# A two-layer hybrid encoder on one core: the attention's last products (weights times values) take precedence over other TensorE work

## The chip, the cores and the metric

One core of a Trainium2 chip runs the whole program in one launch. The metric is the device time of one execution in microseconds (us); a verdict of faster or slower is given from 2% on. TensorE is called PE here, VectorE DVE, ScalarE ACT, GpSimd POOL, and SP is the engine whose queue issues the loads and stores.

## The reference, cut to what matters

```python
for l in range(2):                                   # x is 512 x 1024, float32
    h = rmsnorm(x, g_mix_pre[l])
    a.., b.., c.. = split(h @ w_in[l])
    o_a = gated_deltanet(...)                        # 4 heads of 128, chunks of 64
    o_b = dsa_attention(q, k, v, qi, ki, wi)         # 4 heads of 64, 4 blocks of 128 queries
    o_c = hgrn2(...)                                 # 4 heads of 64
    x = x + rmsnorm(concat([o_a, o_b, o_c]) @ w_out[l], g_mix_post[l])
    h = rmsnorm(x, g_ffn_pre[l])
    x = x + rmsnorm(conv_geglu_ffn(h, ...), g_ffn_post[l])

# of dsa_attention, for one block of 128 queries
score = einsum('bqhs,bqh->bqs', relu(einsum('bqhd,bsd->bqhs', qib, ki)), wib)
_, idx = top_k(score, 128)                           # keys kept for each query
p = softmax(where(valid, q @ k[idx] * 64 ** -0.5, -inf))
o = einsum('bqhk,bqkd->bqhd', p, v[idx])             # weights times values
```

The last line is what the change is about. The kernel computes it with a mask in place of the gather.

## The kernel before

Activations stand with features on partitions and 512 tokens along the free axis. A projection (`project`, lines 179 to 181) multiplies in three passes, high by high, low by high and high by low parts, each a 128x512 product, into a tile `p_mm`; the output projection and the second half of the feed-forward network (`down`, lines 218 to 224) do the same into `p_dn`. These two are called the wide products below.

Each layer runs a mixing part (`mix_phase`) and a feed-forward part. The mixing part computes the projections, the attention (`dsa_*`), the delta rule (`dn_all`) and the gated recurrence (`hg_tile`). `dsa_attend` works on the query blocks in the order 0, 2, 3, 1; block b sees b+1 blocks of 128 keys. For its four heads it computes logits (`p_logit`), the softmax, a transpose of the weights on PE (`p_pT`, line 416) with a copy back by ACT into `lg` (line 417), and then the last products: 4(b+1) of them, 128x128 moving by 64 columns, summed in the tile `p_dsao` (line 420). ACT copies that into `ob` (line 423).

`dn_all` inverts triangular 64x64 blocks from 16x16 pieces: DVE makes `ut` (lines 552, 556) from a piece `u` that SP loads (line 549), PE multiplies 32x32 blocks (`p_l`, 64 of them at line 567 and 64 at 575, with DVE's `z` between, line 568), then 591, 603, 605, 614 and 620, with copies by DVE and ACT between. The recurrence of the delta rule over four chunks follows (`p_u`, `p_S`, `p_dno`, `p_kS`), and next to it the gated recurrence (`hX`, `hkh`, `hqh`, `p_h`, `p_hlo`, lines 693 to 830).

The code is written for a scheduler (the tile framework) that puts each engine's instructions into one fixed order before the run: it takes, of the instructions that are ready by its own account, the one with the best priority. Priority follows the order of the code, and `first(n)` puts what is emitted inside it ahead by `n * 3000` places. Weight splits, evictions of projections and norms already stand in `first`. At run time each engine works its list in that order and waits on semaphores. Wide products that are ready fill the places between the products of the chains.

Places where the order before is shown have lines of the kernel before; the changed kernel has one line more from line 419 on.

Of the kernel before, what the change touches and what calls it, by code (L numbers as in the profile page):

```python
# [19 lines left out]
P = 128  # L20
# [18 lines left out]
def hybrid_encoder_kernel(ctx: ExitStack, tc: tile.TileContext, x, win, wout, wup, wdn, gall, gates,  # L39
                          dncw, ffcw, vecs, hglb, consts, out):  # L40
    nc = tc.nc
    V, S, G, PE, SP = nc.vector, nc.scalar, nc.gpsimd, nc.tensor, nc.sync
# [6 lines left out]
    def first(n=1):  # L49
        return tc.high_priority(offset=n * FIRST)  # L50
# [204 lines left out]
    def mix_phase(l, hid):  # L255
        def alloc(pool, name, tag=None, bufs=1, n=T, dt=F32):
            return pool.tile([P, n], dt, name=name, tag=tag or name, bufs=bufs)

        with ExitStack() as outer:
# [32 lines left out]
            def misc_proj(a):  # L292
                mf = alloc(pool, "mf", tag="hraw", bufs=6)
                with first():
                    S.activation(mf, a, AF.Copy)
                p = ds("misc")
                for b in range(NB):
                    PE.transpose(p[:, b * P:(b + 1) * P], mf[:, b * P:(b + 1) * P], ident)
                mt = alloc(pool, "mt")
                S.activation(mt, p, AF.Copy)  # L300
                return mt.rearrange("p (b c) -> p b c", b=NB)
# [27 lines left out]
            def stacked(a, s, cols, keys, n):  # L329
                PE.matmul(a[:, :n], s[:, cols], keys[0][:, :n], start=True, stop=False)  # L330
                PE.matmul(a[:, :n], s[:, cols], keys[1][:, :n], start=False, stop=True)
# [63 lines left out]
            def dsa_attend(sp, b, qq, keys, misc, bias):  # L395
                n = (b + 1) * P
                qs = slice(b * P, (b + 1) * P)
                lgs = []
                mxs = tiny([4], "mxs")
                for h in range(4):  # L400
                    a = ds("logit")
                    stacked(a, qq[h], qs, keys, n)
                    lg = alloc(sp, "lg", bufs=4)
                    V.tensor_tensor_reduce(lg[:, :n], a[:, :n], bias, 1.0, -3.0e38, OP.add, OP.max, mxs[:, h:h + 1])
                    lgs.append(lg)
                V.tensor_scalar(mxs, mxs, -0.125, None, op0=OP.mult)
                sums = tiny([4], "sums")
                for h in range(4):
                    S.activation(lgs[h][:, :n], lgs[h][:, :n], AF.Exp, scale=0.125, bias=mxs[:, h:h + 1],
                                 accum_out=sums[:, h:h + 1])  # L410
                V.reciprocal(sums, sums)
                for h in range(4):
                    V.tensor_scalar(lgs[h][:, :n], lgs[h][:, :n], sums[:, h:h + 1], None, op0=OP.mult)
                    p = ds("pT")
                    for j in range(b + 1):
                        PE.transpose(p[:, j * P:(j + 1) * P], lgs[h][:, j * P:(j + 1) * P], ident)
                    S.activation(lgs[h][:, :n], p[:, :n], AF.Copy)
                po = po_("dsao")
                for j, h in ((j, 2 * i + r) for i in range(2) for j in range(b + 1) for r in range(2)):
                    PE.matmul(po[64 * (h % 2):64 * (h % 2) + 64, (h // 2) * P:(h // 2 + 1) * P],  # L420
                              misc[:, j, 0:64], lgs[h][:, j * P:(j + 1) * P], start=j == 0, stop=j == b)
                pv = po[:, :2 * P].rearrange("p (i t) -> p i t", i=2)
                S.activation(ob[:, :, qs], pv, AF.Copy)

# [409 lines left out]
            misc = misc_proj(am)  # L834
# [5 lines left out]
            with tc.tile_pool(name="dsa", bufs=1, reuse_waits="tile") as sp:  # L840
                qi = dsa_stack(sp, 0, a0) + dsa_stack(sp, 1)
                keys, ikeys = dsa_keys(sp)
                bias = {0: cst[:, C_B0:C_B0 + P]}
                scores = (None for b in (3, 2, 1) for _ in dsa_score(sp, b, qi, ikeys, cols_[0], bias))
                qq = []
                units = dn_proj()
                for c in DSA_ORDER:
                    if c == "s":
                        next(scores)
                    elif c == "q":  # L850
                        qq += dsa_stack(sp, 4 + len(qq) // 2)
                    else:
                        ts = next(units)
                for _ in scores:
                    pass
                oa = dn_all(ts, cols_)
                for b in (3, 2, 1):
                    dsa_select(bias[b])
                for b in (0, 2, 3, 1):
                    dsa_attend(sp, b, qq, keys, misc, bias[b])  # L860
# [176 lines left out]
```

## Time and profile before

| | us |
|---|---|
| median of the timed runs | 1434.95 |
| the three runs | 1419.99, 1436.18, 1434.95 |
| the profiled execution's own time | 1422.91 |
| its span, first to last instruction | 1420.9 |
| mean granted clock of PE in it | 0.986 |

[...] Durations of PE's products are modelled and overlap: in a row of wide products the next one starts about 0.23 us after the one before, though each is given 0.39 us. An instruction of the code with full float32 operands shows as two records in the profile, so 64 products are 128 records.

### The profile page before, as it was taken

The numbers are of one execution on the slowest core, as the hardware profiler recorded it, in microseconds if no ns is written. First come the engines' busy times: TensorE is split into PE (matmuls) and PEld (weight loads), VectorE is DVE, ScalarE is ACT, GpSimd is POOL, SyncE is SP. The second block draws the span as 40 slices with busy tenths as digits, with TensorE's granted clock in tenths as the row PEclk, the third lists the DMA queues.
The fourth block names the chain that finished last, engine by engine and source line by source line (L and its number), as shares of the span: only waits on it lengthen the run. The fifth ranks groups of instructions, "written<-read, shape, count | busy, mean of one in ns | idle before, by whom it ended". The sixth has DMA issues, their size and how long they took to land.

```text
span 1420.9 us, 19912 instructions
## 1 busy us (share of the span) xinstructions
PE 1372.2 (97%) x7692; PEld 1128.5 (79%) x7692; DVE 912.8 (64%) x1671; ACT 683.9 (48%) x1287; POOL 114.6 (8%) x94
## 2 busy tenths in 40 slices
PE   6999999999999999999999999899999999999998
PEld 6887777778888888888788777688788888888886
DVE  5599977977566656423646998749666665664233
ACT  4355866565444444313543577645554344443132
POOL 2031220110000000000022221102000000000000
PEclk9999999999999999999999999869999999999999
DMA  4423220134423232323333323201353323232332
GB/s 169 124 93 111 94 72 17 60 134 153 161 89 104 91 103 92 102 92 114 136 105 100 97 92 93 56 1 60 133 186 114 103 91 104 89 104 89 104 104 89
DMA packets 50959, 142.93 MB, mean 101 GB/s; under 512 B 14321, under 2 KB 15281, under 8 KB 50865
## 3 DMA queue, kind: packets, MB, share of 16 engines
q1 hardware_dynamic: 50864, 141.66, 30.6%
q8 instruction: 61, 1.00, 0.3%
q14 instruction: 34, 0.27, 0.1%
HBM read 129.29 MB, written 8.95 MB: 97 GB/s over the span
## 4 chain that ended last, share of the span: by engine, by line
PE 75%; DVE 16%; ACT 5%; issue 3%; DMA 1%; DVEq 0%; ACTq 0%
PE p_mm L180 15%; PE p_mm L181 15%; PE p_mm L179 14%; PE p_dn L223 7%; PE p_dn L224 7%; PE p_dn L218 7%; DVE sc L392 3%; DVE m L391 2%; DVE qkv L198 2%; PE p_tp L172 1%; PE p_dsao L420 1%; DVE wlo L123 1%; PE p_hlo L780 1%; ACT whi L122 1%; ACT junk L473 1%
## 5 line engine op out<-in xcount | busy, mean ns | idle before, releaser
L179 PE MATMUL p_mm<-hhi,whi 128*128 128x512 f32 (+1 forms) x1232 | 472.4, 384 | 4.0 <-DVE qkv L198 3.8
L180 PE MATMUL p_mm<-hlo,whi 128*128 128x512 f32 (+1 forms) x1232 | 471.9, 383 | 0.5 <-DVE hlo L176 0.4
L181 PE MATMUL p_mm<-hhi,wlo 128*128 128x512 f32 (+1 forms) x1232 | 472.0, 383 | 0.0
L123 DVE TENSOR_TENSOR wlo<-wraw,whi 128x1024 fp32r<-128x1024 f32 x166 | 204.2, 1230 | 306.1 <-ACT whi L122 304.7
L122 ACT ACTIVATE whi<-wraw 128x1024 fp32r<-128x1024 f32 x190 | 201.4, 1060 | 299.1 <-PE p_mm L180 155.6
L179 PEld LDWEIGHTS p_mm<-hhi,whi 128*128 128x128 f32 x1232 | 233.2, 189 | 47.7 <-ACT qkv L196 4.4
L180 PEld LDWEIGHTS p_mm<-hlo,whi 128*128 128x128 f32 x1232 | 233.4, 189 | 42.6 <-DVE hlo L176 1.1
L181 PEld LDWEIGHTS p_mm<-hhi,wlo 128*128 128x128 f32 x1232 | 233.5, 189 | 42.2 <-issue 0.7
L198 DVE SCALAR_TENSOR_TENSOR u<-p_mm,fcw,u 128x511 f32<-128x511 f32 (+1 forms) x172 | 128.4, 746 | 3.0
L218 PE MATMUL p_dn<-whi,ah 128*128 128x512 f32 x272 | 105.8, 389 | 0.0
L223 PE MATMUL p_dn<-wlo,ah 128*128 128x512 f32 x272 | 105.8, 389 | 0.0
L224 PE MATMUL p_dn<-whi,al 128*128 128x512 f32 x272 | 105.8, 389 | 0.0
L122 ACT ACTIVATE ah<-u 128x512 fp32r<-128x512 f32 x44 | 27.8, 632 | 122.1 <-DVE u L921 122.1
L123 POOL TENSOR_TENSOR wlo<-wraw,whi 128x1024 fp32r<-128x1024 f32 x24 | 57.6, 2400 | 244.6 <-PE p_mm L181 93.0
L920 ACT ACTIVATE u<-u 128x512 f32<-128x512 f32 x44 | 27.8, 633 | 91.8 <-DVE u L198 91.8
L224 PEld LDWEIGHTS p_dn<-whi,al 128*128 128x128 f32 x272 | 51.1, 188 | 10.7
L218 PEld LDWEIGHTS p_dn<-whi,ah 128*128 128x128 f32 x272 | 51.1, 188 | 10.6
L223 PEld LDWEIGHTS p_dn<-wlo,ah 128*128 128x128 f32 x272 | 51.1, 188 | 10.6
L196 ACT ACTIVATE u<-p_mm,fcw 128x512 f32<-128x512 f32 x86 | 57.5, 669 | 0.0
L198 DVE SCALAR_TENSOR_TENSOR qkv<-p_mm,cw,qkv 128x511 f32<-128x511 f32 (+2 forms) x72 | 53.0, 739 | 5.2 <-ACT qkv L196 4.8
L391 DVE MAX8 m<-sc 128x8 f32<-128x512 f32 (+2 forms) x96 | 52.8, 554 | 1.0
L392 DVE MATCH_REPLACE8 sc<-m,sc 128x512 f32<-128x512 f32 (+2 forms) x96 | 51.9, 542 | 0.0
(292 smaller groups left out, 1862.7 us busy)
## 6 DMA issues: line engine op xcount, KB each, us to landing
wraw<-in_wup_dram SPq DMA_DIRECT2D x88, 512.0 KB, 3.4
wraw<-in_win_dram SPq DMA_DIRECT2D x60, 512.0 KB, 3.5
wraw<-in_wdn_dram SPq DMA_DIRECT2D x44, 512.0 KB, 3.4
wraw<-in_wout_dram SPq DMA_DIRECT2D x16, 512.0 KB, 3.4
xd<-xb SPq DMA_DIRECT2D x12, 512.0 KB, 2.7
xb<-xd SPq DMA_DIRECT2D x12, 512.0 KB, 5.5
xb<-in_x_dram SPq DMA_DIRECT2D x8, 512.0 KB, 6.0
g<-in_gall_dram SPq DMA_DIRECT2D x8, 512.0 KB, 4.8
```

Source lines behind the costliest of these rows:

```text
L122: S.activation(hi, src, AF.Copy)
L123: eng.tensor_tensor(lo, src, hi.bitcast(F32), op=OP.subtract)
L179: PE.matmul(out_, ah, bh, start=start, stop=False)
L180: PE.matmul(out_, ah, bl, start=False, stop=False)
L181: return PE.matmul(out_, al, bh, start=False, stop=stop)
L196: S.activation(dst, acc, AF.Copy, scale=w[:, taps - 1:taps])
L198: V.scalar_tensor_tensor(dst[:, s:], acc[:, :T - s], w[:, taps - 1 - s:taps - s], dst[:, s:], op0=OP.mult, op1=OP.add)
L218: first = PE.matmul(acc[b], th[:, bs], piece(hi, i, T), start=k == 0, stop=False)
L223: PE.matmul(acc[b], th[:, bs], piece(lo, i, T), start=False, stop=False)
L224: PE.matmul(acc[b], tl[:, bs], piece(hi, i, T), start=False, stop=k == 2 * npair - 1)
L391: V.max(m8, bias)
L392: V.match_replace(bias, m8, bias, REPL)
```

## The change

The loop of the last products of `dsa_attend` is put inside `first(2)`, so that the scheduler ranks them 6000 places further ahead than before. No instruction, operand or buffer is added or taken away.

```diff
                 po = po_("dsao")
-                for j, h in ((j, 2 * i + r) for i in range(2) for j in range(b + 1) for r in range(2)):
-                    PE.matmul(po[64 * (h % 2):64 * (h % 2) + 64, (h // 2) * P:(h // 2 + 1) * P],
-                              misc[:, j, 0:64], lgs[h][:, j * P:(j + 1) * P], start=j == 0, stop=j == b)
+                with first(2):
+                    for j, h in ((j, 2 * i + r) for i in range(2) for j in range(b + 1) for r in range(2)):
+                        PE.matmul(po[64 * (h % 2):64 * (h % 2) + 64, (h // 2) * P:(h // 2 + 1) * P],
+                                  misc[:, j, 0:64], lgs[h][:, j * P:(j + 1) * P], start=j == 0, stop=j == b)
```

Three places show what the scheduler makes of it.

The first is PE's list in the first layer, at the attention of query block 3 (16 last products, `p_dsao`). Before:

```order
L416 MATMUL p_pT<-cst,lg 128x128 x8
L179 MATMUL p_mm<-hhi,whi 128x512
L180 MATMUL p_mm<-hlo,whi 128x512
L420 MATMUL p_dsao<-lg,mt 64x128
L181 MATMUL p_mm<-hhi,wlo 128x512
L420 MATMUL p_dsao<-lg,mt 64x128 x2
L416 MATMUL p_pT<-cst,lg 128x128 x8
L420 MATMUL p_dsao<-lg,mt 64x128 x13
L330 MATMUL p_logit<-kh,qs 128x256
L331 MATMUL p_logit<-kl,qs 128x256
```

And in the change:

```order
L416 MATMUL p_pT<-cst,lg 128x128 x8
L180 MATMUL p_mm<-hlo,whi 128x512
L421 MATMUL p_dsao<-lg,mt 64x128
L181 MATMUL p_mm<-hhi,wlo 128x512
L179 MATMUL p_mm<-hhi,whi 128x512
L421 MATMUL p_dsao<-lg,mt 64x128 x7
L416 MATMUL p_pT<-cst,lg 128x128 x8
L180 MATMUL p_mm<-hlo,whi 128x512
L181 MATMUL p_mm<-hhi,wlo 128x512
L421 MATMUL p_dsao<-lg,mt 64x128
L330 MATMUL p_logit<-kh,qs 128x256
L331 MATMUL p_logit<-kl,qs 128x256
```

The products of the first two heads now stand together ahead of the second batch of transposes, where most of them stood behind it; 7 of the last 8 stand behind the first pair of logits of the next block.

The second place is PE's list in the first layer some 50 rows later, where `dn_all` begins its 32x32 products. Nothing there is inside `first(2)`; its order changes because the scheduler's choices further up changed. Before:

```order
L181 MATMUL p_mm<-hhi,wlo 128x512
L179 MATMUL p_mm<-hhi,whi 128x512
L567 MATMUL p_l_1405<-ut,Mt 32x32 x32
L567 MATMUL p_l_1439<-ut,Mt 32x32 x32
L575 MATMUL p_l_1473<-ut,z_1045 32x32 x32
L180 MATMUL p_mm<-hlo,whi 128x512
L575 MATMUL p_l_1508<-ut,z_1045 32x32 x32
L591 MATMUL p_l_1550<-tt,Mt 32x32 x8
L181 MATMUL p_mm<-hhi,wlo 128x512
L179 MATMUL p_mm<-hhi,whi 128x512
```

And in the change:

```order
L181 MATMUL p_mm<-hhi,wlo 128x512
L568 MATMUL p_l_1405<-ut,Mt 32x32 x32
L568 MATMUL p_l_1439<-ut,Mt 32x32 x32
L576 MATMUL p_l_1473<-ut,z_1045 32x32 x32
L576 MATMUL p_l_1508<-ut,z_1045 32x32 x32
L592 MATMUL p_l_1550<-tt,Mt 32x32 x8
L179 MATMUL p_mm<-hhi,whi 128x512
L180 MATMUL p_mm<-hlo,whi 128x512
L181 MATMUL p_mm<-hhi,wlo 128x512
```

The wide product between the two halves of the second batch has left; 136 small products follow each other with no wide one among them.

The third place is the same one in the second layer, on PE. Before:

```order
L179 MATMUL p_mm<-hhi,whi 128x512
L180 MATMUL p_mm<-hlo,whi 128x512
L567 MATMUL p_l_7310<-ut,Mt 32x32 x32
L567 MATMUL p_l_7344<-ut,Mt 32x32 x32
L575 MATMUL p_l_7378<-ut,z_6952 32x32 x32
L575 MATMUL p_l_7413<-ut,z_6952 32x32 x32
L181 MATMUL p_mm<-hhi,wlo 128x512
L591 MATMUL p_l_7455<-tt,Mt 32x32 x8
L179 MATMUL p_mm<-hhi,whi 128x512
```

And in the change:

```order
L568 MATMUL p_l_7310<-ut,Mt 32x32 x32
L568 MATMUL p_l_7344<-ut,Mt 32x32 x32
L179 MATMUL p_mm<-hhi,whi 128x512
L180 MATMUL p_mm<-hlo,whi 128x512
L181 MATMUL p_mm<-hhi,wlo 128x512
L179 MATMUL p_mm<-hhi,whi 128x512
L576 MATMUL p_l_7378<-ut,z_6952 32x32 x32
L576 MATMUL p_l_7413<-ut,z_6952 32x32 x32
L592 MATMUL p_l_7455<-tt,Mt 32x32 x8
L180 MATMUL p_mm<-hlo,whi 128x512
L752 MATMUL p_h_8541<-hqh_8470,hkh_8468 64x128 x2
L592 MATMUL p_l_7455<-tt,Mt 32x32 x8
```

Four wide products now stand between the first batch and the second. On DVE, in front of the two copies `z` that release the second batch, the change has this:

```order
L738 TENSOR_TENSOR hX<-hraw 128x256
L739 TENSOR_TENSOR hX<-hraw 128x256
L123 TENSOR_TENSOR wlo<-wraw,whi 128x1024
L569 COPY_PREDICATED z_6952<-cst,p_l_7310 128x256
L569 COPY_PREDICATED z_6952<-cst,p_l_7344 128x256
```

Before, the subtraction of a weight's high part (line 123, `wlo`) stood behind both copies.

## Rows read from the trace of the kernel before

**Rows 1.** Page, part 1: busy time, share of the span and instructions of each engine.

```profile
PE 1372.2 (97%) x7692; PEld 1128.5 (79%) x7692; DVE 912.8 (64%) x1671; ACT 683.9 (48%) x1287; POOL 114.6 (8%) x94
```

**Rows 2.** Page, part 4: the chain that ended last, by engine.

```profile
PE 75%; DVE 16%; ACT 5%; issue 3%; DMA 1%; DVEq 0%; ACTq 0%
```

**Rows 3.** Stages, layer 1 then 2: stretch, its length, busy time, PEclk, DMA share, GB/s.

```profile
171.10:215.91 44.81, 43.08 (x267) 32.58 (x266) 34.68 (x104) 32.19 (x78) 11.42 (x14) 1.00 0.27 72
215.91:308.45 92.54, 86.50 (x986) 70.31 (x987) 76.71 (x164) 56.81 (x98) 8.60 (x5) 1.00 0.13 42
865.70:910.64 44.94, 43.28 (x268) 32.68 (x267) 34.92 (x104) 31.57 (x76) 11.02 (x14) 1.00 0.28 72
910.64:1012.84 102.20, 97.54 (x977) 79.63 (x977) 72.47 (x165) 56.39 (x99) 8.11 (x5) 0.83 0.13 44
```

**Rows 4.** The same view, second layer, where the clock falls and where it returns.

```profile
914.00:916.00 2.00, 1.92 (x124) 1.60 (x125) 1.67 (x5) 1.25 (x5) 0.00 (x0) 1.00 0.04 8
916.00:950.00 34.00, 32.61 (x277) 26.23 (x275) 13.37 (x34) 12.62 (x27) 0.00 (x0) 0.50 0.06 17
950.00:952.00 2.00, 2.00 (x26) 1.82 (x25) 1.91 (x6) 0.57 (x1) 0.00 (x0) 0.97 0.00 0
1059.00:1062.00 3.00, 2.92 (x14) 2.92 (x15) 1.88 (x4) 1.00 (x2) 0.00 (x0) 0.56 0.38 132
```

**Rows 5.** PE in order of time, second layer; in brackets the idle time before and its releaser.

```profile
910.31 0.39 PE L180 MATMUL p_mm<-hlo,whi 128*128 128x512 f32 x1
910.64 1.31 PE L567 MATMUL p_l<-ut,Mt 32*32 32x32 f32 x128
912.67 0.32 PE L575 MATMUL p_l<-ut,z 32*32 32x32 f32 x15 [0.72 <-DVE z L568]
914.08 1.18 PE L575 MATMUL p_l<-ut,z 32*32 32x32 f32 x113 [1.08 <-issue]
915.19 0.49 PE L181 MATMUL p_mm<-hhi,wlo 128*128 128x512 f32 x1
915.66 0.76 PE L591 MATMUL p_l<-tt,Mt 32*32 32x32 f32 x14
917.81 0.31 PE L591 MATMUL p_l<-tt,Mt 32*32 32x32 f32 x2 [1.39 <-issue]
918.05 0.80 PE L179 MATMUL p_mm<-hhi,whi 128*128 128x512 f32 x1
```

**Rows 6.** PE in order of time, the same place in the first layer.

```profile
215.05 0.39 PE L181 MATMUL p_mm<-hhi,wlo 128*128 128x512 f32 x1
215.28 0.39 PE L179 MATMUL p_mm<-hhi,whi 128*128 128x512 f32 x1
215.91 1.31 PE L567 MATMUL p_l<-ut,Mt 32*32 32x32 f32 x128 [0.24 <-DVE ut L556]
218.09 0.75 PE L575 MATMUL p_l<-ut,z 32*32 32x32 f32 x64 [0.88 <-DVE z L568]
218.78 0.49 PE L180 MATMUL p_mm<-hlo,whi 128*128 128x512 f32 x1
...
220.10 0.69 PE L575 MATMUL p_l<-ut,z 32*32 32x32 f32 x59 [0.49 <-issue]
...
220.65 0.63 PE L591 MATMUL p_l<-tt,Mt 32*32 32x32 f32 x15
221.22 0.50 PE L181 MATMUL p_mm<-hhi,wlo 128*128 128x512 f32 x1
```

**Rows 7.** Groups by line, PE, 215.91:308.45: count, busy us, mean ns, idle before.

```profile
L218 PE MATMUL p_dn<-whi,oh 128*128 128x512 f32 x18 | 7.7, 426 | 0.0
```

**Rows 8.** The same groups, PE, 910.64:1012.84.

```profile
L218 PE MATMUL p_dn<-whi,oh 128*128 128x512 f32 x15 | 6.0, 397 | 0.0
```

**Rows 9.** PE in order of time, first layer: transposes and last products of block 3.

```profile
197.81 1.09 PE L416 MATMUL p_pT<-cst,lg 128*128 128x128 f32 x8
198.83 1.90 PE L420 MATMUL p_dsao<-lg,mt 128*64 128x128 f32 x26
200.65 0.39 PE L330 MATMUL p_logit<-kh,qs 128*128 128x256 f32 x1
```

**Rows 10.** The tile p_dsao: who waited for it, us and times.

```profile
  ACT ob L423: 4.1, 4
  DVE hX L701: 3.4, 2
  POOL hqh L697: 2.1, 1
```

**Rows 11.** PE's waits over the span: us in total, times, longest.

```profile
PE p_pT L416 <- DVE lg L413: 5.2, 7, 1.0
```

**Rows 12.** DVE in order of time, second layer: one subtraction of line 123.

```profile
916.15 1.22 DVE L123 TENSOR_TENSOR wlo<-wraw,whi 128x1024 fp32r<-128x1024 f32 x1
```

## The prediction

> **What bounds the kernel now.** I read the page first. PE is busy for 1372.2 of 1420.9 us, 97% [rows 1], and the chain that ended last is PE for 75% and DVE for 16% [rows 2]. So a better order can win PE's idle time, 48.7 us in all, and nothing else, unless PE's work itself takes another time. Its instructions don't change; its clock can. That is why I read the windows by stage next, with the granted clock beside the busy time [rows 3]. The attention's part, up to the first 32x32 product of the delta rule, takes 44.81 us in the first layer and 44.94 in the second, both at a clock of 1.00. The part behind it, up to the end of the gated recurrence, takes 92.54 us at 1.00 in the first layer and 102.20 at 0.83 in the second. In the first, PE idles for 1.73 and 1.66 us; in the second, for 6.04 and 4.66. [...] So I read PE in order of time there, in both layers [rows 5, 6].
>
> **What the low stretch costs.** Both layers do the same work from 215.91 and from 910.64 on, except that the second has done 45 wide products of the output projection by the end of its window (15 on each of three lines) and the first 54 (18 on each) [rows 7, 8]. Nine missing products at the 0.23 us between the starts of two of them [rows 6] are 2.07 us. The stretch therefore cost 102.20 - 92.54 + 2.07 = 11.7 us for 34 us at half clock, about 0.34 us for each us. [...]
>
> **What PE did before it fell.** From the wide product at 910.31 to the one at 918.05, 7.7 us, PE did 32x32 products and a single wide product (915.19), and idled for 0.72 + 1.08 + 1.39 = 3.19 us [rows 5]. In the first layer, from 215.28 to 221.22, 5.9 us, it also had a single wide product (218.78), but idled only for 0.24 + 0.88 + 0.49 = 1.61 us, and the clock stayed [rows 3, 6]. The two differ by little, so I don't take the first layer as safe: in another execution of the same list it may fall too. The profiled time, 1422.91, lies 12.0 us below the median of the timed runs, 1434.95, and one more such stretch is 11.7. That is a guess about runs that no row shows, and the sum is made against 1422.91 alone.
>
> **The change part by part.** *Added and removed work:* none, 0 us.
>
> *The last products themselves.* There are 40 in each layer, and what is moved stays within a few rows. Block 3's 13 products take 1.90 us as 26 records [rows 9], 0.146 us each. In the first layer 5 more of them now stand ahead of the second batch of transposes, 0.73 us, while 7 move behind the first logits of the next block, so those logits start at about the same time. What waits for these products is ACT's copy `ob`, 4.1 us in four times, DVE's `hX`, 3.4 in two, and POOL, 2.1 once [rows 10]; none of these engines is the bound, and wide products cover PE meanwhile. In the second layer the last group shrinks from 7 to 4 products, so `hX` may start 3 x 0.146 = 0.44 us earlier. The bounds: no more can be won up to the delta rule than PE's idle time there, 1.73 + 1.66 = 3.4 us [rows 3]; the nearest row for a loss is PE's wait for the scaled weights, 5.2 us in seven times [rows 11], which could at worst come once more. As wide products stand around every one of these places, I take -0.4 us.
>
> *The start of the delta rule, first layer.* The change takes the one wide product out of the middle. The durations of rows 6 for what is left: 1.31 us for the first batch, 0.75 + 0.69 for the second, 0.63 for 8 products of line 591, 3.4 in all, plus waits of 1.6 us (first layer) to 3.2 (second): 5.0 to 6.6 us with no wide product at all. In length that lies around the two stretches we have, and in wide products it is below both. I put the chance that the clock falls here at 0.8, for 0 to 17.5 us (half as much again as 11.7) and most likely about 11.7: the list goes on with 3 and 6 wide products between the small ones, where the low stretch of the second layer had 8 and 5.
>
> *The start of the delta rule, second layer.* Four wide products, 0.92 us at 0.23, now split the two batches, which covers the wait of 0.72 behind the first. Against that, DVE now does a subtraction of 1.22 us [rows 12] just ahead of the copies `z`, so that a wait of up to 1.22 - 0.92 + 0.72 = 1.0 us comes back. Behind it stand 0.32 + 1.18 us of the second batch, 1.08 + 1.39 of waits that the old order had, and 0.76 of line 591 [rows 5]: 2.3 to 5.7 us without a wide product, then one, then 16 more small ones and 4 products `p_h`. This is a coin toss, 0.5; where the clock holds, 11.7 us come back.
>
> *The rest.* The order of the recurrences behind it changes in hundreds of rows, with the same products and the same number of wide ones to fill with. PE idles for 6.04 + 4.66 = 10.7 us there [rows 3]. I take 0 and keep 4 us on either side. The dip at 1059 [rows 4], 3 us at 0.56, I leave as it is, at about 1.7 us; it can go or come again in the first layer.
>
> **The sum for the likeliest case.** One long low stretch, now in the first layer, and none in the second: 1422.9 - 0.4 + 11.7 - 11.7 = 1422.5; with some idle time saved where the four wide products cover the wait of 0.72 us, 1422. If it falls in the second layer alone, the time is the same. Its own range is 1416 to 1428 (4 us for the rest, and half of the 11.7 if the first layer's stretch is shorter or longer).
>
> **The rivals.**
>
> *Both layers fall.* For it: the first layer has lost its wide product, and the second keeps a long stretch with few. Against it: the four products in the second. It gives 1422 + 11.7 = 1434, which happens to be the median before. [...]
>
> *Neither falls.* For it: in the first layer the clock held with 1.61 us of idle time [rows 6], and the second layer gets the four products. It gives 1422 - 11.7 = 1410.
>
> *Slower than before: the clock stays down.* In rows 4 it came back only when the small products had ended. If in both layers it fell at the first 32x32 products and stayed low to the end of the gated recurrence, 92.54 us in the first layer and 68 more than now in the second (102.20 - 34), at 0.34 us each, that would be 31 + 23 = 54 us: 1477. It decides from some 120 more low us on, which is 41 us. Against it: wide products stand in this part in numbers (74 and more), and the clock came back among them.
>
> *The change doesn't do what it says.* Nearly the same rows for `p_dsao`, with the same wide products about them: the clock then behaves as before, in the second layer alone, and the time is 1421 to 1423.
>
> **How the numbers follow.** Taking the two falls as independent: first layer alone 0.8 x 0.5 = 0.40, second alone 0.2 x 0.5 = 0.10, both 0.40, neither 0.10. I take something off each for the last two rivals: one stretch 0.47, both 0.37, neither 0.09, clock stays down 0.03, nothing moves 0.04. The prediction is the likeliest, **1422**. The range goes from 1408 (neither, with 2 us of idle time won) to 1438 (both, with 4 us lost) and leaves out the long stretch and the tails. A measurement of this kernel can tell about 2% from no change, 28.7 us: below 1406.3 or above 1463.6. All the idle time of the touched stages (14.1 us) and the clock's 13.4 together would be needed to reach 1395 from 1422.9, so faster has 0.03; slower has the third rival's 0.03; within 2%: 0.94.
>
> **What would show it right or wrong.** In the changed profile PE has again 7692 instructions and about 1372 us of busy time, more by what the clock adds. The attention's part takes 44 to 45 us in both layers. The windows show a clock of 0.5 beginning within 7 us of the first `p_l` of the first layer (5.3 in the second before), and in the second either none or one as before; the time follows at 0.34 us for each low us. Wrong would be: a stage before the delta rule that is longer by more than 3 us (then the last products did take something away from the softmax), idle time of PE behind it above 15 us in all, or a time that differs by more than 5 us from 1422.9 while the low us are the same.

## The result and the profile after

The changed kernel takes 1430.68 us in the median of 14 runs (1426.2 to 1440.13), the kernel before 1424.85 in the median of 14 (1417.45 to 1437.01). The ratio is 1.0073 (95% interval 1.0045 to 1.0102): under 2%, but the whole interval lies above 1. I had forecast 1422. Here and below, ratios, means and counts leave out executions more than 1.5% above the fastest of the same kernel. The profiled execution took 1431.65 us (span 1429.70), against 1422.91 (span 1420.90) before.

PE's busy time on the page of the changed kernel, where [rows 1] had 1372.2 us:

```profile
PE 1377.0 (96%) x7692; PEld 1132.6 (79%) x7692; DVE 916.4 (64%) x1671; ACT 683.2 (48%) x1287; POOL 112.5 (8%) x94
```

The instructions are as many as before. Now the stages of [rows 3], with the stretch between the layers and the one behind the second layer's recurrence (stretch, its length, busy time by engine, granted clock as a share of full speed, DMA share, GB/s), of the changed kernel:

```profile
171.00:219.24 48.24, 44.14 (x262) 32.98 (x262) 36.94 (x102) 30.99 (x76) 10.71 (x14) 0.96 0.24 67
219.24:314.42 95.18, 90.27 (x990) 73.75 (x990) 77.01 (x166) 58.42 (x100) 7.71 (x5) 0.96 0.13 41
314.42:876.22 561.80, 551.16 (x2597) 456.76 (x2595) 344.62 (x561) 253.22 (x472) 36.89 (x25) 0.99 0.34 112
876.22:922.63 46.41, 44.88 (x271) 33.87 (x270) 36.61 (x108) 33.12 (x81) 11.61 (x14) 1.00 0.25 69
922.63:1023.19 100.56, 94.15 (x972) 77.09 (x972) 72.28 (x161) 54.65 (x96) 7.46 (x5) 0.85 0.15 49
1023.19:1429.70 406.51, 398.95 (x1837) 332.12 (x1836) 214.83 (x272) 158.15 (x250) 0.00 (x0) 1.00 0.33 109
```

and the two stretches that [rows 3] lacks, of the kernel before:

```profile
308.45:865.70 557.25, 547.90 (x2596) 453.78 (x2595) 344.86 (x561) 253.60 (x472) 37.12 (x25) 1.00 0.34 113
1012.84:1420.90 408.06, 400.33 (x1836) 333.23 (x1835) 215.07 (x272) 158.60 (x250) 0.00 (x0) 0.99 0.33 110
```

Stage by stage the change brings +3.43, +2.64, +4.55, +1.47, -1.64 and -1.55 us; together 8.9, less 0.1 for the start that lies a little earlier: the 8.8 by which the span grew. Three things make it up.

*A wait of the attention in the first layer.* PE in order of time, and DVE and POOL at that place (changed kernel; idle time before and releaser in brackets):

```profile
207.45 0.39 PE L179 MATMUL p_mm<-hhi,whi 128*128 128x512 f32 x1
211.09 0.70 PE L416 MATMUL p_pT<-cst,lg 128*128 128x128 f32 x4 [3.25 <-DVE lg L413]
```

```profile
204.72 3.53 DVE L406 TENSOR_SCALAR mxs<-mxs 128x4 f32<-128x4 f32 x1
204.84 3.41 DVE L544 TENSOR_TENSOR prod<-ln 128x169 f32<-128x169 f32 x1
208.31 0.33 DVE L546 TENSOR_REDUCE ln<-prod 128x13 f32<-128x169 f32 x1
```

```profile
203.12 0.96 POOL L694 MEMSET hA<- 128x1024 f32 x1 [22.87 <-PE p_logit L331]
...
207.71 0.52 POOL L698 MEMSET hqh<- 128x512 f32 x1
```

DVE's scaling of four maxima, 128x4 elements, lasts until 208.25, and POOL's last of nine memsets in a row ends at 208.23. The 3.25 us for which PE then waited are most of the +3.43.

*More short stretches at half clock.* In both profiles PE's granted clock is 1.00 or 0.50, and a value between is the mean of a stretch that has both. It is at 0.50 for 3.4 us each at 212, 226, 294, 359 and 704, none of which the kernel before had in its profile; its dip at 1059 [rows 4] is gone. The first lies in the stage with +3.43, the next two in the one with +2.64, the last two in the one with +4.55, and the missing dip in the one with -1.55.

*The long stretch in the second layer is still there*, 30.7 us instead of 34:

```profile
929.10:959.80 30.70, 29.36 (x271) 23.35 (x272) 10.39 (x28) 12.25 (x24) 0.00 (x0) 0.50 0.01 2
```

What PE did before it fell (changed kernel, second layer; compare [rows 5]):

```profile
922.64 1.31 PE L568 MATMUL p_l<-ut,Mt 32*32 32x32 f32 x128
923.88 0.50 PE L179 MATMUL p_mm<-hhi,whi 128*128 128x512 f32 x1
...
925.67 1.31 PE L576 MATMUL p_l<-ut,z 32*32 32x32 f32 x128 [0.60 <-DVE z L569]
927.61 0.34 PE L592 MATMUL p_l<-tt,Mt 32*32 32x32 f32 x5 [0.62 <-DVE tt L578]
930.45 0.79 PE L592 MATMUL p_l<-tt,Mt 32*32 32x32 f32 x11 [2.50 <-issue]
```

The four wide products stand between the two batches, as the order said. But the two "issue" waits of [rows 5], 1.08 and 1.39 us, are gone; in their place stands one of 2.50, from 927.95 to 930.45, behind the fifth record of line 592, and the clock falls inside it, at 929.10.

### The profile page after: what moved, and what is told of

Same layout as the page of the kernel before. It is cut to its first block, busy times and chain, and to the rows that moved or that the text cites. A ratio compares the mean times of both kernels' runs of the same rounds, so it can differ in the third digit from the quotient of the medians.

```text
span 1429.7 us, 19913 instructions
## 1 busy us (share of the span) xinstructions
PE 1377.0 (96%) x7692; PEld 1132.6 (79%) x7692; DVE 916.4 (64%) x1671; ACT 683.2 (48%) x1287; POOL 112.5 (8%) x94
## 3 DMA queue, kind: packets, MB, share of 16 engines
q1 hardware_dynamic: 50864, 141.66, 30.7%
## 4 chain that ended last, share of the span: by engine, by line
PE 76%; DVE 15%; ACT 4%; issue 3%; DMA 1%; POOL 0%; DVEq 0%; ACTq 0%; POOLq 0%
PE p_mm L180 15%; PE p_mm L181 15%; PE p_mm L179 15%; PE p_dn L224 7%; PE p_dn L223 7%; PE p_dn L218 7%; DVE sc L392 3%; DVE m L391 2%; DVE qkv L198 1%; DVE wlo L123 1%; PE p_dsao L421 1%; PE p_tp L172 1%; PE p_hlo L781 1%; ACT junk L474 1%; PE p_pT L416 1%
```

## The experiments

For every execution the mean granted clock is known, and with it, as the two profiles above show the levels 1.00 and 0.50 alone, the time at half clock: (1 - clock) x 2 x span. A clock of 0.985 over 1425.7 us is 43 us "at 0.5". The table gives its mean, beside that of the kernel before on the same chip, and how many of the executions compared had under 30 us. In the kernel before these were 91 of 121.

| kernel | ratio to before (95%) | us at 0.5 | before | under 30 us |
|---|---|---|---|---|
| the change, first chip | 1.0073 (1.0045-1.0102) | 50.9 | not known | 0 of 14 |
| after_again | 1.0112 (1.0051-1.0172) | 57.3 | 21.6 | 0 of 6 |
| after_l406_two_inputs | 1.0091 (1.0055-1.0128) | 51.2 | 21.6 | 0 of 12 |
| after_first_layer_only | 1.0045 (1.001-1.0081) | 35.3 | 21.6 | 5 of 12 |
| after_second_layer_only | 1.0063 (1.003-1.0095) | 44.4 | 21.6 | 0 of 12 |
| after_kept_busy | 0.9984 (0.995-1.0017) | 15.4 | 25.4 | 10 of 11 |
| before_kept_busy | 1.001 (0.9972-1.0048) | 28.7 | 25.4 | 7 of 12 |
| after_kept_busy_more | 0.9993 (0.996-1.0026) | 16.7 | 25.4 | 8 of 9 |
| after_wide_in_a_run | 1.0118 (1.007-1.0166) | 33.9 | 20.8 | 3 of 6 |
| before_wide_in_a_run | 1.0103 (1.0065-1.014) | 39.7 | 20.8 | 2 of 9 |
| before_l406_two_inputs | 1.0051 (1.002-1.0081) | 37.0 | 20.8 | 4 of 12 |
| after_kept_busy_l406 | 0.9987 (0.9954-1.002) | 13.7 | 20.8 | 11 of 12 |
| before_same | 0.9994 (0.9958-1.0029) | 25.8 | 24.5 | 10 of 12 |
| after_first_layer_again | 1.003 (0.9991-1.0068) | 39.6 | 24.5 | 4 of 9 |
| after_kept_busy_second | 1.0107 (1.0055-1.0158) | 63.7 | 24.5 | 0 of 6 |
| after_eight_in_a_run | 1.0082 (1.005-1.0114) | 44.5 | 24.5 | 3 of 11 |
| after_shift_16 | 1.0035 (0.9998-1.0072) | 23.5 | 21.4 | 9 of 11 |
| after_shift_32 | 1.0038 (0.9999-1.0077) | 33.2 | 21.4 | 6 of 12 |

**Is it the hold-up of DVE, and which layer?** The first four runs are the change again, L406 in another form, and the precedence in one layer alone, twice.

> The changed kernel as it is, for a second profile. In the first one VectorE's scaling of the four maxima (the tensor_scalar on mxs, L406, 128x4) began at 204.72 us and ended at 208.25, 3.53 us instead of 0.60 in the kernel before, while GpSimd ran nine memsets in a row from 203.12 to 208.23; TensorE then waited 3.25 us for the softmax. Theory S (VectorE is held by GpSimd's memsets, and the order of instructions puts it there): the same again, L406 over 3 us at about 204.7, the p_pT wait over 3 us, ratio to the kernel before 1.004 to 1.010. Rival C (a chance of that one execution; the loss is the granted clock alone): L406 0.2 to 0.6 us in the second profile, p_pT waits of 5 us in all as before, and the same ratio from stretches at 0.5 clock elsewhere.

> The changed kernel with the scaling of mxs (L406) written as mxs*(-1.125)+mxs, an operation with two inputs, instead of a tensor_scalar with one; no engine's order of instructions moves by a row. Theory S (the one-input form is what GpSimd's memsets hold up): L406 takes 0.2 to 0.3 us, the 3.25 us wait on p_pT in the first layer falls to under 1 us, the first p_l starts at about 216 us instead of 219.24, and the time falls by 3.3 us, up to 5 with one short stretch at 0.5 clock (1.7 us) that came right after the wait: ratio 1.002 to 1.005. Rival O (the wait comes from the order, the last products ahead of the logits, whatever form L406 has): wait and ratio as in the changed kernel, 1.004 to 1.010 around 1.007. Rival M (memsets hold any operation there, the 128x169 product beside it too): L406 is short, but the product or the next operation takes 3 us and the wait stays.

```diff
-                V.tensor_scalar(mxs, mxs, -0.125, None, op0=OP.mult)
+                V.scalar_tensor_tensor(mxs, mxs, -1.125, mxs, op0=OP.mult, op1=OP.add)
```

> The precedence for the last products in the first layer alone; the second layer has its old order around the attention. Theory S (the loss is the hold-up in the first layer and what the clock does behind it): L406 held for over 3 us, ratio 1.004 to 1.009, as the full change. Rival 2 (the loss sits in the second layer, whose long stretch at 0.5 clock stays): ratio 0.998 to 1.002.

```diff
-                with first(2):
+                with first(2) if l == 0 else ExitStack():
```

> The precedence in the second layer alone; the first layer has its old order. Theory S: no hold-up of L406, the first p_l at about 216 us, ratio 0.997 to 1.003, with a long stretch at 0.5 clock of about 31 us in the second layer still there. Rival 2 (the loss sits in the second layer): ratio 1.004 to 1.009.

The edit is the same with `l == 1`. In the second profile of the change L406 took its usual time and the first `p_l` stood at 216.56, as early as before (215.91); yet the ratio was 1.0112. So the hold-up was a chance of the first profile, theory S is out as the cause, and rival C holds. The edit of L406 could then show nothing: no profile taken on this chip has a hold-up to remove. What the four kernels show together is the line on which all their executions lie: with 0.43 us taken off for each us at 0.5, the means are 1407.2 (before), 1407.9 (change), 1408.0 (L406), 1407.4 (first layer) and 1407.8 (second). The order itself costs under 1 us; all the rest is the clock. Fitted for itself, the price is 0.42 in the 29 executions of the kernel before, and 0.39 to 0.45 on the four other chips used later. Of the added us at 0.5, the first layer alone brings 14, the second alone 23.

**Does more dense work keep the clock up?** Twelve wide products that nobody reads, six in each layer, behind the first two batches of the solve, in both orders; then twenty; and the kernel before for a second profile.

> The changed kernel with twelve extra 128x512 products whose result nobody reads: in each layer three behind the first 128 products of 32x32 of the delta rule's solve (L568) and three behind the next 128 (L576), where TensorE waits for VectorE. In the four kernels of the first batch the time of every run was 1407 to 1408 us plus 0.43 us for each us at 0.5 clock, whatever the order; the mean of the us at 0.5 was 22 for the kernel before and 51 to 57 with the change. Theory K (the whole loss is the 0.5 clock, which begins where TensorE has only 32x32 products and waits): the extra products cost 12 x 0.23 = 2.8 us at the most, about half of it inside waits of 0.85 and 3.1 us, and the us at 0.5 fall to 20 or fewer: 1408 + 9 + 1, ratio to the kernel before 0.996 to 1.003 where the change alone has 1.009 to 1.011. Rival O (the order costs by itself, the clock only follows waits): the ratio stays at 1.007 or more and rises by up to 0.002.

```diff
+                kw = do("kw")
+                def warm(n, after):
+                    for _ in range(n):
+                        m = PE.matmul(kw, hid.hi[0][:, 0, 0:P], hid.hi[0][:, 0, :], start=True, stop=True)
+                        tc.add_manual_dep(m.ins, after.ins.name, mybir.DependencyInfo(
+                            mybir.DependencyClass.NoSync, mybir.DependencyReason.DATA), reason="order")
...
+                    if g == 1:
+                        warm(3, lp)
```

> The kernel before with the same twelve extra products at the same places, for whether the clock is a cost there too. Theory K: the us at 0.5 fall from a mean of 22 to about 8, worth 6 us, less 1 to 2 for the products: ratio 0.995 to 0.999, and the runs lie closer together than the 1411 to 1429 of the kernel before. Rival O: ratio 1.000 to 1.002, with the same spread.

> The changed kernel with the twelve extra products and, in each layer, one more behind each of the second pair of 32x32 batches (L606, one for each of its two banks) and each half of the first 64x64 batch (L615), 20 in all. Theory K: if stretches at 0.5 are left between L606 and L621 in the kernel with twelve, they go, and the time is 0 to 4 us under that kernel's; if none are left, it is 1 to 2 us longer (8 x 0.23 = 1.8). Rival O: longer by 2 us in any case.

> The kernel before as it is, for a second profile. Theory K: in the second layer the clock falls to 0.5 within 10 us of the first p_l, as in the first profile (916), but returns after about 7 us where the thirteen wide products that stand in two runs (eight and five) between the p_l batches follow, if this is one of its more frequent, shorter runs; the stage's length is 21.7 us plus 0.44 for each us at 0.5. Rival O: the stage takes 34 us again.

With the twelve products the loss was gone: 15 us at 0.5 instead of 51 to 57, and 0.9984, with the last products still ahead. In the order of before they did nothing (28.7 beside 25.4), which theory K had not expected; eight more in the changed kernel added nothing either. The second profile of the kernel before took 34.5 us for the second layer's solve, with 34 at 0.5 again, so it was not one of the frequent, shorter runs. It also had the hold-up of L406, in the old order (DVE, kernel before, second profile):

```profile
204.24 3.82 DVE L406 TENSOR_SCALAR mxs<-mxs 128x4 f32<-128x4 f32 x1
```

**Is it the scattering of the wide products?** A real reordering, no work added: one projection's wide products in a run between L576 and L592; and L406 once more.

> The changed kernel, no instruction more or less, with one projection's wide products (128x512, those of the second half of the first gate) put in a run: in each layer they follow the solve's second 32x32 batch (L576), and its third (L592) waits in TensorE's order for the eighteenth of them. In the changed kernel's second layer 15 wide products stand between the first p_l and the first p_u, four of them ahead of the second batch and the other eleven singly or in threes and fours; in the kernel before 19, most of them in a run of eight and one of five. Theory K (few and scattered wide products keep the clock at 0.5 there): the second layer's stretch at 0.5 falls from 31 us to 10 or fewer, the mean per run from 51 to 57 us to 25 or fewer, ratio to the kernel before 0.996 to 1.003 without any extra work. Rival O (the order of the last products costs by itself): ratio 1.007 or more. Rival D (the run delays the solve, and what hangs on it waits): the stretch at 0.5 shrinks, and the ratio stays over 1.004.

```diff
+                    if run and k == 1:
+                        put_after(last, solve["before"])
+                    if run and k == 5:
+                        put_after(solve["after"], last)
```

`put_after` sets the first behind the second in PE's order; `solve` holds the last product of L576 and the first of L592, `last` is the wide product of step k.

> The same run of wide products in the order of the kernel before. Theory K: the mean at 0.5 falls from 22 to 25 us to 15 or fewer: ratio 0.994 to 0.999. Rival D: 1.000 to 1.005. In the kernel before with twelve extra products the mean did not fall (28.7), so a ratio of 1.000 would say again that in this order the clock falls at another place than these products cover.

> The kernel before with the scaling of mxs (L406) written with two inputs; no order moves. In the second profile of the kernel before L406 was held from 204.24 to 208.06 us, as in the first of the changed kernel; so it happens in both orders, in some executions. Theory S2 (a chance meeting with GpSimd's memsets, worth 3.5 us when it happens): where the time less 0.43 us for each us at 0.5 scatters by 2.4 us in the kernel before, as on two of the three chips so far, it scatters by 1 here and its mean is 1 to 2 us lower: ratio 0.998 to 1.000. Where it scatters by 0.9 in the kernel before, no difference. Rival: the same scatter of 2.4 in both.

> The changed kernel with the twelve extra products and L406 with two inputs. Theories K and S2: ratio 0.994 to 0.999 (0.9984 for the twelve alone, less 1 to 2 us where the meeting occurs). Rival: 0.998 to 1.002, as without the second edit.

Rival D won. The clock stayed up through the second layer's solve, yet that stage took 32.06 us in the profile (from the first `p_l` to the first `p_u`) instead of some 21 at full clock (20.69 in the first layer of the kernel before), which I put down to the solve's now waiting for the run, and the time less 0.43 for each us at 0.5 rose by 9.5 us; in the order of before, by 5.4. `before_l406_two_inputs` is a miss that I cannot explain: no row moved, the hold-up's scatter was 1.3 us with and without it, and yet 37 us at 0.5 instead of 21. The next run measured whether two loads of one program can differ so.

**Load, first layer, and two tests in the second layer.**

> The kernel before, unchanged, as if it were another kernel: how far two loads of the same program differ. If the us at 0.5 clock scatter in the same way in every load: ratio 0.998 to 1.002, mean at 0.5 of 20 to 25 us as in the runs beside it. If a load has a habit of its own (the edit of L406 alone, which moved no row, rose to a mean of 37 us and a ratio of 1.005): a ratio off 1.000 by 0.003 to 0.006, with the difference wholly in the us at 0.5.

> The precedence in the first layer alone, once more: the first time it gave 1.0045 (1.001 to 1.0081), a mean of 35 us at 0.5, no more than the edit of L406 that moves no row. Theory K2 (only the second layer's order costs anything that can be told from chance): executions with under 26 us at 0.5 in a third of the cases or more, ratio anywhere from 0.999 to 1.005, not beyond what the unchanged kernel shows beside it by more than 0.003. Rival (both layers cost the same): 1.0045 again, 0.004 or more above the unchanged kernel.

> The changed kernel with six extra products, three behind L568 and three behind L576, in the second layer alone; the first layer is the changed kernel's. Theory K2: all 44 executions so far with the precedence in the second layer had 31 us or more at 0.5, of which 30.7 in one stretch there; with that stretch gone the lowest runs have 3 to 12 us and the mean is 20 to 28, 0.43 x 28 = 12 us less than the change: ratio 0.998 to 1.003. Rival (the six products only shift the stretch): no execution under 25 us, ratio 1.007 or more.

> The changed kernel with eight extra 128x512 products in one run, in the second layer alone, behind the first sixteen products of L592, when the clock has already fallen. In the profile of the first-layer-only kernel (old order in the second layer) the clock returned at 927.4 right after a run of eight wide products, in the changed kernel's order no run is longer than four and it stayed at 0.5 for 30.7 us. Theory K2: the clock falls as before and returns behind the run: 7 to 14 us in the stretch instead of 31, of which a gain of 7 to 10 us is left less 8 x 0.23 to 0.43 = 2 to 3.5 for the products: ratio 1.001 to 1.006. Rival (what keeps the clock down is not the want of a run): the stretch stays at 25 us or more, ratio 1.009 to 1.013.

```diff
+                    if g == 0 and l == 1:
+                        warm(8, lp)
```

(`lp` is the last product of L592's first half.)

The unchanged kernel repeats itself (0.9994, 25.8 beside 24.5). The first layer alone adds 15 us at 0.5, as it added 14 before, so it does have a share of the loss, against theory K2. `after_kept_busy_second` was the useful miss. Its six products stood where they should, and the clock fell all the same (PE, that kernel, second layer; L586 and L604 are the old L576 and L592, `p_kw` the extra products):

```profile
928.84 0.96 PE L566 MATMUL p_kw<-hhi 128*128 128x512 f32 x3
929.64 0.39 PE L179 MATMUL p_mm<-hhi,whi 128*128 128x512 f32 x1
930.65 1.31 PE L586 MATMUL p_l<-ut,z 32*32 32x32 f32 x128 [0.62 <-DVE z L579]
931.89 0.96 PE L566 MATMUL p_kw<-hhi 128*128 128x512 f32 x3
932.78 0.24 PE L604 MATMUL p_l<-tt,Mt 32*32 32x32 f32 x2
935.47 0.78 PE L604 MATMUL p_l<-tt,Mt 32*32 32x32 f32 x14 [2.44 <-issue]
```

The clock went to 0.5 at 935.76 for 30.7 us, right behind a wait of 2.44 us for no tile at all. The kernel with extra products in both layers has no such wait there (PE, `after_kept_busy`, same place):

```profile
918.67 1.50 PE L586 MATMUL p_l<-ut,z 32*32 32x32 f32 x128 [0.77 <-DVE z L579]
920.10 0.97 PE L566 MATMUL p_kw<-hhi 128*128 128x512 f32 x3
921.00 0.69 PE L604 MATMUL p_l<-tt,Mt 32*32 32x32 f32 x16
```

`after_eight_in_a_run` shows the other end of the stretch: the wait of 2.27 us is there, the clock falls, and it returns within the run of eight, after 6.8 us instead of 30.7 (its windows; the run is at 940.12 to 943.46):

```profile
928.94:935.90 6.96, 4.30 (x266) 3.40 (x265) 6.87 (x18) 3.46 (x9) 0.00 (x0) 1.00 0.26 80
935.98:942.80 6.82, 6.16 (x38) 4.74 (x39) 2.18 (x6) 3.51 (x6) 0.00 (x0) 0.50 0.01 2
942.80:954.15 11.35, 11.30 (x217) 9.30 (x215) 4.29 (x11) 5.95 (x13) 0.00 (x0) 1.00 0.01 3
```

Its ratio, 1.0082, is above the 1.001 to 1.006 expected: less is saved than the first layer and the eight products take.

**What the wait is, and whether it makes the stretch.** The DMA of the changed kernel from 927.95 to 929.10, in the wait of 927.95 to 930.45, and then in the 4.45 us ahead of it (queue, kind: packets, MB, share):

```profile
q8 instruction: 1, 0.02, 5.1%
q1 hardware_dynamic: 17, 0.02, 4.9%
```

```profile
q1 hardware_dynamic: 127, 0.50, 37.1%
```

A packet of instructions ran from 928.10 to 929.03, and PE went on 1.42 us behind it. Of 42 "issue" waits in the solves of all twenty profiles, the two shifted kernels' included, each ended 1.25 to 1.60 us behind the end of such a packet. And in [rows 5] 113 + 1 + 14 records of products lie from the first wait to the second: 128, the length of one batch, which takes 1.31 us. So it seems that PE waits for its own instructions, and that they come in lots of about 128 such records: that is my estimate from these counts, and no trace shows the lots themselves. In the changed kernel such a wait takes 2.50 us.

The traces say two things more. Counted from the start of the program, every "issue" wait of the second layer's solve stands at PE's product record 5020 to 5024 or 5149 to 5152, in every order: the place in the stream stays, and the order decides which product stands there. And in the changed kernel the packet for the second place started 2.37 us after PE had passed the first, behind the load of 0.50 MB above, with the DMA engines busy for a share of 0.74 (the last column but one):

```profile
925.73:928.10 2.37, 1.60 (x133) 1.37 (x133) 2.31 (x7) 0.77 (x2) 0.00 (x0) 1.00 0.74 225
914.08:915.12 1.04, 1.04 (x113) 1.04 (x113) 0.75 (x2) 0.38 (x2) 0.00 (x0) 1.00 0.00 0
```

The second line is the same stretch of the kernel before, from its first wait's end to the packet: 1.04 us, with no load. In the seven profiles with such a load in between it is 1.9 to 2.5 us, in the thirteen others 1.12 at most. That the load holds the packet up is read from this, and was not tested. The place was tested: the stream was shifted with the solve's order left alone.

> The changed kernel with sixteen 32x32 products (32 in TensorE's records, under 1 us in all) ahead of the second layer's first transposes (p_misc), 190 us before the solve; they write what the transposes overwrite. No row moves in the solve on any engine; only TensorE's instructions stand 32 places later in their stream. In every profile an 'issue' wait of TensorE in the solve ends 1.3 to 1.5 us after a packet of instructions (queue q8) has landed, and in the second layer of the changed kernel it is one wait of 2.3 to 2.5 us at the sixth product of L592, in the order before two of about 1 us. Theory F (TensorE waits for its instructions, and where it does depends on where blocks of the stream begin): the wait moves ahead by 32 products, into L576, or changes its length by more than 0.5 us; if this wait alone keeps the clock down, executions under 26 us at 0.5 appear and the mean falls below 45. Theory K2 (the clock stays down for want of a run of wide products, whatever the wait): the wait moves, the stretch in the second layer stays at 25 us or more, no execution is under 28, ratio 1.007 to 1.012. Rival R (the wait is for an operand of L592): 2.5 us at the same product, nothing changes.

```diff
                 p = ds("misc")
+                for _ in range(16 if l == 1 else 0):
+                    PE.matmul(p[0:32, 0:32], ident[0:32, 0:32], ident[0:32, 0:32], start=True, stop=True)
```

> As the kernel with sixteen, with thirty-two products (64 in TensorE's records). Theory F: the wait moves ahead by 64 products or more, or becomes two shorter ones, and executions under 26 us at 0.5 appear if it is what keeps the clock down. Theory K2: the stretch at 0.5 in the second layer stays at 25 us or more in the profile and no execution is under 28, ratio 1.007 to 1.012. Rival R: 2.5 us at the sixth product of L592, as in the changed kernel.

Theory F holds for the wait. In both the place of the wait is 32 and 64 records ahead, behind the 101st and the 69th record of the second batch, and there PE stops for 0.28 and 0.22 us from one start to the next, 1.37 and 1.42 us behind the end of a packet; no wait of 2 us is left in the second layer (PE, `after_shift_16`, the two sides of its place, then `after_shift_32`; L570, L578 and L594 are the old L568, L576 and L592):

```profile
936.79 1.08 PE L578 MATMUL p_l<-ut,z 32*32 32x32 f32 x101 [0.95 <-DVE z L571]
937.95 0.44 PE L578 MATMUL p_l<-ut,z 32*32 32x32 f32 x27
```

```profile
935.76 1.31 PE L570 MATMUL p_l<-ut,Mt 32*32 32x32 f32 x128
...
938.78 1.52 PE L578 MATMUL p_l<-ut,z 32*32 32x32 f32 x128 [0.58 <-DVE z L571]
940.72 0.69 PE L594 MATMUL p_l<-tt,Mt 32*32 32x32 f32 x16 [0.41 <-DVE tt L580]
```

In `after_shift_32` the solve, with the same rows in the same order but for a few neighbours that changed places, ran at full clock to its end:

```profile
935.76:945.00 9.24, 8.22 (x322) 6.38 (x321) 8.34 (x21) 6.88 (x16) 0.00 (x0) 1.00 0.20 62
945.00:955.54 10.54, 10.42 (x191) 8.27 (x190) 5.67 (x15) 6.13 (x13) 0.00 (x0) 1.00 0.01 2
```

It took 19.78 us, against 32.41 in the changed kernel. The one profile of `after_shift_16`, of its slowest execution (1442.23 us), shows the opposite. Its rows stand just as in the changed kernel, and without the long wait the clock fell all the same, for as long, and the solve took 30.18 us:

```profile
938.70:969.40 30.70, 30.68 (x281) 24.68 (x282) 12.40 (x33) 12.38 (x25) 0.00 (x0) 0.50 0.02 6
```

So the long wait is not needed for the stretch. What the shift changed is how often it comes: executions with under 30 us at 0.5, of which there were none in 50 with the precedence in the second layer and the long wait (the change, `after_again`, L406, second layer alone, `after_kept_busy_second`), are 9 of 11 and 6 of 12 with the shift (on a chip on which the change itself was not run). Theory K2 falls as the whole account, since the scattered wide products were still there; that a run of wide products brings the clock back once it has fallen, `after_eight_in_a_run` still speaks for, with 6.8 us instead of 30.7 in its one profile.

The old order did not keep its clock either. In all six profiles that have it in the second layer, with no extra products and no wide products put in a run (the kernel before three times, with the L406 edit, and the first layer alone twice) it fell in that solve, for 34.1 us in two and 6.8 in four; with the wait of 2.3 to 2.5 us it fell in six of six, for 30.7 us in five and 6.8 in the one with the run of eight. The new order lost the early return; what decides about that return is not shown.

The ratios, 1.0035 and 1.0038, look like those of the first layer alone, 1.0045 and 1.003, but are made up differently. With thirty-two products the us at 0.5 (33.2) are as the first layer alone has them (35 and 40). With sixteen they are nearly those of the kernel before (23.5 beside 21.4), and the time less 0.43 for each us at 0.5 is 3 us above it; the extra products take 1.19 us of that in the profile, and the rest is not explained.

## Why the prediction was wrong

*PE bounds, instructions unchanged, the clock can change.* Right: 7692 instructions again, 4.8 us more busy time, and nearly the whole loss is clock (on the second chip all but 0.7 us).

*The price of low time.* Mis-sized. I took 0.34 us for each us at 0.5 from two unlike stages and the 34.00 us at 0.50 in [rows 4]; within one order, over many executions, it is 0.39 to 0.45. The 1.7 us that I put on the dip at 1059, and with it the 13.4 of the clock, was an estimate that no run shows: at the measured price its 3.4 us at 0.50 come to 1.3 to 1.5.

*The last products, -0.4 us.* In the first layer right without the hold-up (216.56 in the second profile, where the stage before it is as long as before). The sign I had named for "wrong", a stage before the delta rule longer by over 3 us, did appear, but not for the reason I gave: DVE's operation of 128x4 took 3.53 us, and 3.82 in the second profile of the kernel before, so in either order, by chance. In the second layer the stage is 1.47 us longer, with 271 PE records instead of 268 and 1.60 us more busy time; wide products stand ahead of the delta rule that stood behind it, so part of this is moved, not lost.

*First layer: the clock falls with 0.8, most likely for 11.7 us of time.* The direction was right: it fell in all nine profiles with the first layer's new order that have no extra product there, for 3 to 34 us at a time. But the old order falls in some executions too, so what counts is the difference, 14 to 15 us at 0.5, some 6 us where I had put 11.7.

*Second layer: a coin toss, with 11.7 us to come back where the clock holds.* This is the step that failed. I set 0.5, on the ground that four wide products cover the wait behind the first batch, and took the two "issue" waits over as "1.08 + 1.39 of waits that the old order had". They are not properties of those rows. They stand at fixed places of PE's stream, records 5020 to 5024 and 5149 to 5152, and each ends 1.25 to 1.60 us behind a packet of instructions; in the new order one of 2.3 to 2.5 us stood in the place of the two, in all six profiles that have neither the shift, nor the wide products put in a run, nor extra products in both layers. With it the 50 executions above all had 30 us or more at 0.5, where 91 of 121 of the kernel before had less. Nor was there much to come back: the base for the 11.7 us was a stretch of 34 us, which the old order had in two of six profiles. Instead of winning 11.7 us or nothing, the new order in the second layer alone cost 23 us at 0.5, a ratio of 1.0063, some 9 us. That the wait is there and that shifting it away restores most executions, 15 of 23, is shown; that the wait itself brings the clock down is not, since in one profile the clock fell without it.

*The rest, 0 within 4 us.* Held: from the first `p_u` to the last `p_hn` it is 70.84 us before and 71.65 after in the first layer, 66.37 and 67.12 in the second.

*The sum.* With both layers falling, my rival "both layers fall" gave 1434 (I gave it 0.37), for 1430.68 measured. The outcome was on the list, but not the wait behind it; what was wrong was its chance, and the likeliest case traded one stretch for another that did not go away. That 1434 lies within 4 us of the measured time is in part luck: it is reckoned from 1422.91 with 11.7 us for the first layer, where the two layers cost some 6 and 9. The guess that one more such stretch separates the executions of the kernel before held on the second chip: they lie from 1410 to 1429 us, with 8 to 51 us at 0.5, on one line.

*Still open.* Why the first layer's share arises: its "issue" wait is 0.7 to 1.3 us in the profiles with the new order and up to 0.5 in those with the old, which fits the same cause, but its stream was not shifted. Why a fall lasts 6.8 us in some executions and over 30 in others. Whether a shift of the kernel before, one that puts a long wait into its solve, would cost it the same. Why the edit of L406 alone raised the us at 0.5. And since twelve extra products also shift the stream, `after_kept_busy` does not show which of the two helped; `after_kept_busy_second` speaks for the shift. No version was faster than the kernel before beyond its interval.

## What to carry to other kernels

When an order changes around dense batches of very small products, an "issue" wait in the old trace need not stay as it is: here two of 1.08 and 1.39 us became one of 2.50, at another product. Look whether a packet of instructions ends shortly before it does (here 1.25 to 1.60 us), count the products between two such waits (here 128 records), and see what else the DMA engines carry then (here a load of 0.50 MB). Compare the time at half clock over many executions before explaining one profile: here one profile showed a 3.25 us wait that was chance in both orders, and hid the cause. A shift of the stream by a few useless instructions is a cheap test that leaves the order alone: here sixteen products of 1.19 us in all.

## What the hardware did that I had not expected

Without the shift, all 50 executions with the long wait had 30 us or more at half clock. With sixteen 32x32 products placed 190 us ahead, 1.19 us of work, 2 of 11 had; with thirty-two, 6 of 12.

A 128x4 operation on DVE took 3.53 and 3.82 us while POOL ran memsets back to back; the same happened in the second layer of three other profiles (3.53 us each), and in none of the three profiles with the two-input form. As it came in five of the 34 places with the one-input form, none in six proves little. In both first-layer cases the operation ended 0.02 us behind the last memset (208.25 and 208.23, 208.06 and 208.04), so it spanned the rest of a run of memsets, not one of 0.52 us. That the memsets held it was not shown: in the first profile of the kernel before the same operation, at 203.68 in the midst of the same memsets, took 0.60 us.
